# A new hand-written order for the last part of layer two, with one more wait between the halves of a bank

## The chip, the core and the metric

The kernel runs on one core of one Trainium2 chip. The metric is the device time of one execution in microseconds. The median of three runs before the change is 786.66 us (784.89 to 787.54).

## The reference

The kernel computes one inference step of a two-layer decoder trunk for a prompt of 512 tokens and a group of 8 x 4 sample tokens that share all weights. Layer one mixes tokens by dilated sliding-window attention; layer two, where the change lies, by a matrix-state recurrence (RWKV-7). Both layers also attend to 256 memory tokens, gate the branches and project them out. Cut to layer two:

```python
p = xn @ w_in                                   # one input projection
cols, q_mem, gate = split(p)
xs = cols + mu * (prev(cols) - cols)            # token shift
r, k, v, w, a = heads(xs)                       # 12 heads of 64
for t in tokens:                                # per head, state S is 64 x 64
    sa = S @ a_t
    S = S * w_t + outer(sa, b_t) + outer(v_t, k_t)
    y_t = S @ r_t
y = group_norm(y) + (r * k * r_k).sum() * v
h = concat([y, cross_attention(q_mem)]) * silu(gate)
out = x + rms_norm(h @ w_out)
```

## The kernel before

All arithmetic is in 32 bits. A large product is made as three matmuls of a high and a low part: `hi` is a rounded copy of the weights (ScalarE, line 328), `lo` the rest (GpSimd, line 329).

The recurrence of layer two is worked in chunks of 64 tokens, 8 chunks, for three groups `g` of four heads. For one group the steps are these.

- Scores, and then `products` (line 1506, `P2` for the last group): a triangular inverse by elimination. VectorE makes 30 steps of two operations, an outer product `TX` (line 1557) and its addition to `T` in PSUM (line 1559). Steps 1 to 7 of the last group belong to the part ahead; steps from 8 on (`HOLD`) belong to the part that the change orders. After steps 12 and 22 a small square `n` for the sample tokens (line 1541) is put in. After step 30, `T` is transposed on VectorE (line 1569), two small products `X` (lines 1579 and 1589) complete the inverse, and `w`, `q` and `v` (lines 1600 and 1615) apply it.
- `Chunks(2)` (`C`): for chunk c, `inputs` (line 1789) multiplies the state by the chunk's columns (`z`) and VectorE adds the result to `UV` (line 1795); `state` (line 1801) makes the next state `St` (`z` again, then VectorE at line 1812), with `Sd`, the decayed state, from GpSimd (line 1799).
- `outputs` (`Y`): y of two chunks at a time, in two halves that write one PSUM bank: a first half of few matmuls for i = 0, 2, 4, 6 and a second half for i = 1, 3, 5, 7 (`y_of`, line 1760). The matmuls of a second half wait for a VectorE operation of the step that follows the first half (line 1779).
- `block` (`N0`, `N1`, `N2`): the group norm of the y just made (`yc`, `gst`, transposes `gn` by TensorE, `bv`) and the gate (`ug`, line 1929, then `h` on ScalarE and GpSimd).

Beside it stand the output projections. `earlier` (`F`) makes the products `o` of the first four feature blocks, 16 products of six 128x512 matmuls (by half, token tile and group) and sample products `o100s` to `o111s`; VectorE adds each to `z` (lines 2134 and 2139). `F` steps left over from `crossed` come first. `weights` (`W`) splits the weight pieces, `inner` (`U`) gates two more blocks, `residuals` (`R`) transposes the residual (`x`, line 2001; ScalarE copies it out at line 2002). `last` (`O0` to `O3`) makes the last products of a token tile, squares them (line 2033), scales (line 2040) and adds the residual (line 2045); `last_sample` (`L`) does it for the sample rows (`o20s`, `o21s`, `zS`). `S2` and `M2` are the sample tokens of the last group.

What sets the order: up to this part a planner (`Flow.run`) does. From there on `Flow.close` takes the next step of the stream that the written list `CLOSE` names, and each of TensorE, VectorE, ScalarE and GpSimd executes its instructions in that order. Each engine takes its own queue in order, so an instruction that waits holds up all behind it. A stream may `yield` the name of an event, and the list has to reach that event first. The products share two PSUM banks (`mm`), as do the residual transposes; the small products, the norms' transposes and the sample steps share one bank (`q`).

Of the kernel before, what the change touches and what calls it, by code (L numbers as in the profile page):

```python
# [13 lines left out]
SYNC = DependencyInfo(DependencyClass.Sync, DependencyReason.DATA)  # L14
# [39 lines left out]
PRELOAD = ()  # L54
MULT = 'GGGGGGDD'
LOWER = 'GGGGGG'
CLOSE = 'F F F W1 W1 W1 P2 P2 P2 P2 F P2 P2 P2 F P2 R R F F W W P2 F F P2 F F P2 F F P2 P2 R W P2 W1 P2 R R F W1 W1 U U U W W P2 R F P2 F P2 U U P2 F P2 F P2 F F P2 W W F P2 F W F F R P2 F F P2 W W P2 F F P2 F F F P2 P2 F P2 P2 P2 P2 W W P2 F P2 P2 C C C F C C S2 S2 S2 F F Y Y Y Y C Y Y Y C W F C C Y Y W W F C Y Y Y N0 N0 C N0 F C F F Y Y Y N0 F C C Y Y Y N0 N1 N1 C F N0 N1 F C N0 N0 N1 F N1 C N1 Y Y Y F F N0 N0 N0 C C N1 N1 Y Y Y S2 N2 N2 O0 O0 O0 N1 N2 S2 O1 O1 O1 O0 N2 O1 S2 O0 N1 N1 S2 S2 O1 O0 O0 O1 S2 O2 O2 O2 S2 N2 O2 O1 O0 O0 S2 O2 O2 O0 O0 O1 O1 S2 S2 O1 O1 R M2 R N2 O2 N2 N2 R N2 R R N2 N2 M2 O2 O1 C O2 O0 O2 O2 M2 M2 L L L L O3 O3 O3 O3 O1 O1 O3 O3 L L O2 O2 O2 O3 O3 O3 L L O3 O3 L C C L L L O0 O0 O3 O3 O3 L L'
YB = [[[0, 4], [4, 8]], [[0, 4], [4, 8]], [[0, 4], [4, 6], [6, 8]]]
QUARTERS = (1, 1), (0, 0), (1, 0), (0, 1)
QO = (0, 2, 1, 3)  # L60
# [122 lines left out]
class Flow:  # L183
# [47 lines left out]
    def close(self):  # L231

        with self.tc.manual_schedule(engines={ET.PE, D, A, G}):
            for name in CLOSE.split():
                s = next(s for s in self.streams if s.name == name)
# [19 lines left out]
def _device(tc, I, O):  # L255
# [32 lines left out]
    def ps_zs(name):  # L288
        return psum[0].tile([128, 1024], F32, tag="zs", bufs=1, name=name)

    def ps_c(tag, name, bufs=1):
        return psum[0].tile([128, 512], F32, tag=tag, bufs=bufs, name=name)
# [419 lines left out]
    with ExitStack() as pro:  # L712
# [44 lines left out]
        for j, g in enumerate(GORD):  # L757
            a = 1152 + 32 * j
# [259 lines left out]
    half = {}  # L1018
# [189 lines left out]
    flow = Flow(tc)  # L1208
# [92 lines left out]
    def unit(c, j, h):  # L1301
        a = ((c - j) % 8 // 2 * 2 + h) * 64
        return H2[(c + j) % 2], slice(a, a + 64)


    def turned(c, j, h):
        return h ^ (c + j) % 2

    def score(c, j, h):
        a = ((c - j) % 8 // 2 * 2 + turned(c, j, h)) * 64  # L1310
        return H2[(c + j) % 2], slice(a, a + 64)
# [350 lines left out]
    def add_affine(p, src, cols, shape):  # L1662
        o_ = bvs[p][:, cols]
        o_ = o_.rearrange("p (c t) -> p c t", t=64) if shape else o_
        nc.vector.scalar_tensor_tensor(o_, src, vec("lnw", p), o_, ALU.mult, ALU.add)
# [80 lines left out]
    class Chunks:  # L1746

        def __init__(self, g):
            self.g, self.st = g, sts[g]
            self.states, self.c, self.yps, self.norms, self.fence, self.n, self.ops = [], 0, None, [], False, 0, []  # L1750
            self.St = rw.tile([128, 2, 64], F32, tag="St", bufs=4, name=f"St{g}i")
            nc.vector.memset(self.St, 0.0)
            self.states.append(self.St)
            self.zs = ps_zs(f"z{g}").rearrange("p (e k c v) -> p e k c v", k=2, c=4, v=64)
# [5 lines left out]
        def y_of(self, cs, e):  # L1760


            g, (AR, SR, UV, u) = self.g, (self.st.AR, self.st.SR, self.st.UV, self.st.u)
            a, b = [ab for ab in YB[g] if ab[0] <= cs[0] < ab[1]][0]
            if cs[0] == a and e:
                self.yps = ps_c("y", f"y{g}_{a}")
            yps = self.yps
            steps = [(c, k, t) for c in cs for k in range(3) for t in range(2) if (c or k) and (k == 0 and t) == e]
            for step in steps:
                c, k, t = step  # L1770
                for j, h in PAIRS:
                    if turned(c, j, h) == t:
                        r, s = score(c, j, h)
                        lhs = SR[r, 2 - k, j, s] if k else AR[H2[h], j, 1, CH[c]]
                        rhs = (UV[r, 1, j, unit(c, j, h)[1]] if k == 1 else u[r, c, t] if k else self.states[c][H2[h], j ^ h])
                        y = ((c - a) * 2 + h) * 64
                        self.put(yps[r, y:y + 64], lhs, rhs, e and step == steps[0], not e and step == steps[-1])
                        if not e and self.fence:
                            tc.add_manual_dep(flow.last(), self.ops[self.begun if g == 2 else -1].name, SYNC, reason="one half of a bank")
            c = cs[1]  # L1780
            if not e and c == b - 1:
                def out(pt):
                    pt = pt[:, 0:(b - a) * 128].rearrange("p (c j t) -> p c j t", j=2, t=64)
                    for j in range(2):
                        add_affine(2 * g + j, pt[:, :, j], slice(64 * a, 64 * b), True)

                self.norms.append(norm(g, yps, 2 * (b - a), f"_{b}", out, self.fence))
# [306 lines left out]
    def closing():  # L2094
# [65 lines left out]
        def outputs():  # L2160
            yield "chunks"
            C = out.chunks
            for i in range(8):
                c = i + 1
                yield f"step{2 * c - 2 + c % 2}"
                if i % 2:
                    yield f"step{n + 1}"
                else:
                    if [i] == [b for _, b in YB[2] if b == i]:
                        yield f"read{i}"  # L2170
                n = C.n
                if c % 2:
                    C.begun = n
                C.y_of((c - 1, c) if c % 2 else (c - 2, c - 1), c % 2 == 1)
                flow.done(f"turn{i}")
                yield
# [17 lines left out]
        flow.spawn(0, inner(), name="U")  # L2194
        flow.spawn(0, earlier(), name="F")
        flow.spawn(0, outputs(), name="Y")
        for i, (a, b) in enumerate(YB[2]):
            flow.spawn(0, block(i, a, b), name=f"N{i}")
# [103 lines left out]
```

## Time and profile before

| | |
|---|---|
| median of 3 runs | 786.66 us |
| profiled execution, its own time | 787.78 us |
| its span | 785.9 us |
| granted TensorE clock over the span | 0.986 |
| TensorE busy | 744.5 us, 95% |
| VectorE busy | 448.0 us, 57% |
| GpSimd busy | 354.4 us, 45% |
| ScalarE busy | 342.0 us, 44% |

Times in rows of the profile are microseconds from the start of the span. A row of the timeline has start, length, engine, line, operation, what it writes and reads, and in brackets how long the engine stood idle before it and which instruction ended that. PE is TensorE, DVE is VectorE, ACT is ScalarE, POOL is GpSimd. The part that the list orders fills about the last 110 us.

### The profile page before, as it was taken

The page shows a single profiled execution, that of the slowest core. Times are in us where ns is not written, and L with a number is a line of the kernel's source. Part 1 is how long each engine was busy: PE and PEld are TensorE (multiplying, and loading weights), DVE is VectorE, ACT ScalarE, POOL GpSimd, SP SyncE. Part 2 cuts the span into 40 slices and gives each one's busy share as a digit, 9 for nine tenths or more (in the row PEclk, how much of TensorE's full clock was granted, in tenths as well). Part 3 has the DMA queues.
Part 4 walks back from the last instruction along what each step waited for, and adds up shares of the span by engine and source line. Part 5 has one row for each costly group of instructions (what it writes and reads, how often), then busy time and mean ns, then how long its engine had stood idle before and what let it go on. Part 6 is the DMA issues. An engine that isn't in the chain of part 4 may idle for free.

```text
span 785.9 us, 20504 instructions
## 1 busy us (share of the span) xinstructions
PE 744.5 (95%) x8457; PEld 622.5 (79%) x8457; DVE 448.0 (57%) x1076; ACT 342.0 (44%) x807; POOL 354.4 (45%) x385
## 2 busy tenths in 40 slices
PE   6899999999999999999999999999999999989894
PEld 5877868888986877798888889888897888657763
DVE  7733321216646376662444679644799457777566
ACT  7554321214554364447585358223644242533122
POOL 4642322332240393655443338533855444333465
PEclk9999999999999999999999999899999999999997
DMA  7465358872133772263114522201222341622003
GB/s 254 126 204 200 108 172 278 318 279 98 63 116 117 250 233 75 69 198 103 54 49 148 166 80 80 71 16 33 80 73 83 112 112 56 185 93 84 17 15 132
DMA packets 58785, 98.21 MB, mean 125 GB/s; under 512 B 7775, under 2 KB 23039, under 8 KB 58655
## 3 DMA queue, kind: packets, MB, share of 16 engines
q1 hardware_dynamic: 58692, 96.91, 37.7%
q8 instruction: 66, 1.08, 0.6%
q14 instruction: 27, 0.22, 0.1%
HBM read 83.39 MB, written 13.49 MB: 123 GB/s over the span
## 4 chain that ended last, share of the span: by engine, by line
PE 67%; DVE 15%; POOL 5%; DMA 5%; ACT 3%; issue 3%; SPq 0%; DVEq 0%; POOLq 0%; ACTq 0%
PE o L1941 3%; PE Sx L591 2%; PE b_h L337 2%; PE y L1757 2%; PE b_h L336 2%; PE b_h L338 2%; DVE TX L1557 1%; PE z L1757 1%; PE sc L1473 1%; PE ox L615 1%; DMA raw_a<-in_w_in_a 1%; PE o L832 1%; PE ptx L607 1%; DVE T L1559 1%; PE w L1600 1%
## 5 line engine op out<-in xcount | busy, mean ns | idle before, releaser
L329 POOL TENSOR_TENSOR lo_a<-raw_a,hi_a 128x512 fp32r<-128x512 f32 x44 | 56.9, 1295 | 124.1 <-ACT hi_a L328 123.4
L329 POOL TENSOR_TENSOR lo_b<-raw_b,hi_b 128x512 fp32r<-128x512 f32 x58 | 78.5, 1354 | 73.4 <-ACT hi_b L328 62.4
L328 ACT CAST hi_a<-raw_a 128x512 fp32r<-128x512 f32 x44 | 27.3, 620 | 64.3 <-DMA raw_a<-in_w_in_a 36.5
L328 ACT CAST hi_b<-raw_b 128x512 fp32r<-128x512 f32 x58 | 36.4, 628 | 31.8 <-issue 9.9
L336 PE MATMUL b_h<-xg,hi_b 128*128 128x272 f32 x160 | 47.9, 300 | 0.0
L337 PE MATMUL b_h<-xg,lo_b 128*128 128x272 f32 x160 | 47.2, 296 | 0.0
L338 PE MATMUL b_h<-xg,hi_b 128*128 128x272 f32 x160 | 47.1, 295 | 0.0
L1941 PE MATMUL o<-hi_o,h 128*128 128x512 f32 x96 | 36.0, 426 | 2.9 <-DVE z L2134 2.3
L337 PEld LDWEIGHTS b_h<-xg,lo_b 128*128 128x128 f32 x160 | 30.1, 188 | 2.3 <-issue 1.9
L1559 DVE TENSOR_TENSOR T<-T,TX 128x30 f32<-128x30 f32 (+14 forms) x90 | 30.1, 335 | 2.2
L336 PEld LDWEIGHTS b_h<-xg,hi_b 128*128 128x128 f32 x160 | 30.1, 188 | 1.3 <-ACT hi_b L328 0.4
L1557 DVE TENSOR_TENSOR TX<-T,TT 128x30 f32<-128x30 f32 (+14 forms) x90 | 29.2, 325 | 3.3 <-ACT T L1528 1.7
L338 PEld LDWEIGHTS b_h<-xg,hi_b 128*128 128x128 f32 x160 | 30.1, 188 | 0.9 <-issue 0.5
L1941 PEld LDWEIGHTS o<-hi_o,h 128*128 128x128 f32 x96 | 18.8, 196 | 9.3 <-DVE z L2134 2.8
L329 POOL TENSOR_TENSOR lo_o<-raw_o,hi_o 128x512 fp32r<-128x512 f32 x12 | 15.7, 1316 | 22.1 <-ACT hi_o L328 14.8
L1799 POOL TENSOR_TENSOR Sd<-St,DF 128x128 f32<-128x128 f32 x21 | 8.9, 422 | 36.6 <-DVE St L1812 25.0
L1941 PE MATMUL o<-lo_o,h 128*128 128x512 f32 x48 | 19.7, 411 | 0.9 <-POOL lo_o L329 0.9
L1382 POOL TENSOR_TENSOR rv<-rv,mhalf 128x10 f32<-128x10 f32 x6 | 14.2, 2374 | 13.8 <-DVE rv L1381 7.7
L1473 PE MATMUL sc<-AR,BK 64*64 64x128 f32 x384 | 18.4, 278 | 1.9 <-DVE bv L1419 0.9
L824 ACT COPY PT<-pa 128x512 f32<-128x512 f32 x16 | 9.0, 586 | 18.7 <-PE pa L823 14.7
L1933 POOL TENSOR_TENSOR h<-ug,h 128x128 fp32r<-128x128 f32 (+3 forms) x11 | 9.1, 838 | 17.1 <-ACT h L1932 17.0
L1473 PEld LDWEIGHTS sc<-AR,BK 64*64 64x64 f32 x384 | 12.6, 132 | 5.2 <-issue 1.8
(1112 smaller groups left out, 2732.3 us busy)
## 6 DMA issues: line engine op xcount, KB each, us to landing
raw_b<-in_w_in_b SPq DMA_DIRECT2D x58, 256.0 KB, 2.9
raw_a<-in_w_in_a SPq DMA_DIRECT2D x44, 256.0 KB, 2.9
kc<-in_kc SPq DMA_DIRECT2D x18, 512.0 KB, 6.3
vc<-in_vc SPq DMA_DIRECT2D x18, 512.0 KB, 6.9
raw_o<-in_w_out_b SPq DMA_DIRECT2D x16, 256.0 KB, 2.6
out_win<-t SPq DMA_DIRECT2D x12, 272.0 KB, 3.4
x<-in_x SPq DMA_DIRECT2D x8, 272.0 KB, 5.2
xr<-in_x SPq DMA_DIRECT2D x16, 136.0 KB, 4.1
```

Source lines behind the costliest of these rows:

```text
L328: nc.scalar.copy(hi, raw)
L329: lo_eng.tensor_tensor(lo, raw, hi.bitcast(F32), ALU.subtract)
L336: nc.tensor.matmul(ps[:, :n], hi, xh, start=first, stop=False)
L337: nc.tensor.matmul(ps[:, :n], lo, xh, start=False, stop=False)
L338: nc.tensor.matmul(ps[:, :n], hi, xl, start=False, stop=last)
L591: nc.tensor.matmul(S[hh][64 * e:64 * e + 64, 0:256], qm[r, f, a:a + 64], kT[l][r, f, :], start=True, stop=True)
L1382: nc.gpsimd.tensor_tensor(rv[:, 1], rv[:, 0], mhalf.to_broadcast([128, 10]), ALU.pow)
L1473: nc.tensor.matmul(pts[e][unit(c, j, h)[0], a:a + 128], BK[H2[h], j, x, CH[c]], AR[H2[h], j, :, CH[c]], start=True, stop=True)
L1557: nc.vector.tensor_tensor(pd, TP[:, 0:s, s:s + 1].to_broadcast([128, s, w]), TT[:, s:s + 1, s + 1:32].to_broadcast([128, s, w]), ALU.mult)
L1559: nc.vector.tensor_tensor(TP[:, 0:s, s + 1:32], TP[:, 0:s, s + 1:32], pd, ALU.add)
L1757: nc.tensor.matmul(out, lhs, rhs, start=start, stop=stop)
L1941: nc.tensor.matmul(ps, x, w, start=begun is None and i + k == 0, stop=i == len(hs) - 1 and k == 2)
```

## The change

The list `CLOSE` is written in another order. It has the same steps, and three more `Y`: `outputs` now also yields once before the first halves for i = 2, 4 and 6, until the step after the last second half is in the list. With it goes a new wait: the matmuls of these first halves wait for the VectorE operation of that step (`ended`), as those of the second halves already do (`begun`).

```diff
-CLOSE = 'F F F W1 W1 W1 P2 P2 P2 P2 F P2 P2 P2 F P2 R R F F W W P2 F F P2 F F P2 F F P2 P2
...
+CLOSE = 'W1 W1 P2 P2 P2 P2 P2 P2 P2 P2 P2 P2 P2 P2 P2 P2 W1 P2 F F F F P2 P2 P2 F F W1 F
...
-            self.states, self.c, self.yps, self.norms, self.fence, self.n, self.ops = [], 0, None, [], False, 0, []
+            self.states, self.c, self.yps, self.norms, self.fence, self.n, self.ops, self.ended = [], 0, None, [], False, 0, [], None
...
-                        if not e and self.fence:
-                            tc.add_manual_dep(flow.last(), self.ops[self.begun if g == 2 else -1].name, SYNC, reason="one half of a bank")
+                        if self.fence and not (e and self.ended is None):
+                            op = self.ops[(self.ended if e else self.begun) if g == 2 else -1]
+                            tc.add_manual_dep(flow.last(), op.name, SYNC, reason="one half of a bank")
...
                 if i % 2:
                     yield f"step{n + 1}"
-                else:
+                elif i:
+                    yield f"step{n + 1}"
+                    C.ended = n
                     if [i] == [b for _, b in YB[2] if b == i]:
                         yield f"read{i}"
```

Where instructions move, engine by engine. The changed file has up to three lines more, so L1757 to L1779 keep their numbers, and L1941, L1950, L2134 and L2001 are L1942, L1951, L2135 and L2002 in it.

VectorE in the elimination, before: steps 11 to 14 (a step is the row pair L1557, L1559; the last numbers count the step and its width), the add of the first output product (`z<-z,o`) and the copy of the first small square.

```order
L1559 TENSOR_TENSOR T_8643<-T_8643,TX_8637 128x11x20
L2134 TENSOR_TENSOR z_8986<-z_8986,o_9153 128x512
L1557 TENSOR_TENSOR TX_8637<-T_8643,TT_8636 128x228
L1559 TENSOR_TENSOR T_8643<-T_8643,TX_8637 128x12x19
L1548 COPY TX_8637<-n_9175 32x64
L1557 TENSOR_TENSOR TX_8637<-T_8643,TT_8636 128x234
L1559 TENSOR_TENSOR T_8643<-T_8643,TX_8637 128x13x18
L1557 TENSOR_TENSOR TX_8637<-T_8643,TT_8636 128x238
L1559 TENSOR_TENSOR T_8643<-T_8643,TX_8637 128x14x17
L2134 TENSOR_TENSOR z_8987<-z_8987,o_9186 128x512
```

VectorE in the elimination, now, around the place where the first add stands: steps 20 to 22, with the norm's multiply (`yc`) and the sample square's addition (`SAs`).

```order
L1557 TENSOR_TENSOR TX_8637<-T_8643,TT_8636 128x220
L1559 TENSOR_TENSOR T_8643<-T_8643,TX_8637 128x20x11
L1642 TENSOR_TENSOR yc_8_8309<-yc_8_8309,gst_8_8308 128x512
L1557 TENSOR_TENSOR TX_8637<-T_8643,TT_8636 128x210
L1559 TENSOR_TENSOR T_8643<-T_8643,TX_8637 128x21x10
L2135 TENSOR_TENSOR z_8986<-z_8986,o_9194 128x512
L1557 TENSOR_TENSOR TX_8637<-T_8643,TT_8636 128x198
L1559 TENSOR_TENSOR T_8643<-T_8643,TX_8637 128x22x9
L1546 TENSOR_TENSOR SAs_7543<-SAs_7543,n_9204 32x64 x2
```

The first add stood behind step 11 and stands behind step 21 now; the multiply stood ahead of step 8. Between step 8 and the transpose stood eight adds of 128x512, two of 128x128 and the gates of two blocks; now there are five and one, no gate, and the multiply.

TensorE at the start of the recurrence, before: `v`, the first state's `z`, a sample product, and the next `inputs` and `state` with nothing between them.

```order
L1615 MATMUL v_9620<-UV_7540,SA_7538 64x64 x16
L1757 MATMUL z_9640<-UV_7540,BK_6994 64x64 x8
L1950 MATMUL o110s<-hi_o_9373,xsm 32x128 x4
L1950 MATMUL o110s<-lo_o_9374,xsm 32x128 x4
L1950 MATMUL o110s<-hi_o_9399,xsm 32x128 x4
L1950 MATMUL o110s<-lo_o_9400,xsm 32x128 x4
L1757 MATMUL z_9640<-St_0_9649,AR_6993 64x64 x4
L1757 MATMUL z_9640<-UV_7540,BK_6994 64x64 x8
L1682 MATMUL q2s<-UVs_7542,SAs_7543 32x64 x4
```

TensorE there, now: the third of four output products that stand in the first steps, between `inputs` (reads `St_0`) and `state` (reads `BK`).

```order
L1757 MATMUL z_9568<-St_0_9577,AR_6993 64x64 x4
L1942 MATMUL o_9606<-hi_o_9375,h_9118 128x512
L1942 MATMUL o_9606<-lo_o_9376,h_9118 128x512
L1942 MATMUL o_9606<-hi_o_9375,h_9118 128x512
L1942 MATMUL o_9606<-hi_o_9526,h_9118 128x512
L1942 MATMUL o_9606<-lo_o_9527,h_9118 128x512
L1942 MATMUL o_9606<-hi_o_9526,h_9118 128x512
L1757 MATMUL z_9568<-UV_7540,BK_6994 64x64 x8
```

The four output products of the second group's first half stood ahead of `w`, around the two `X`; all four now stand behind `v`.

TensorE at its end, before: residual transposes (`x`, `x1s`), the last state's `z`, and the first of the last two token products.

```order
L2001 MATMUL x_10176<-ident,x1SA 128x128 x4
L2007 MATMUL x1s<-ident,last 32x128 x8
L1757 MATMUL z_9640<-UV_7540,BK_6994 64x64 x8
L1651 MATMUL gn2s<-ident,yc2s 64x64 x2
L1941 MATMUL o_10231<-w2h,h_9118 128x512
L1941 MATMUL o_10231<-w2l,h_9118 128x512
```

TensorE at its end, now: the last token product's end, then transposes, then the sample products.

```order
L1942 MATMUL o_10200<-w2h,h_9118 128x512
L1651 MATMUL gn2s<-ident,yc2s 64x64 x2
L2002 MATMUL x_10215<-ident,x1BK 128x128 x4
L2002 MATMUL x_10221<-ident,x1SA 128x128 x4
L2008 MATMUL x1s<-ident,last 32x128 x8
L1951 MATMUL o20s<-w2h,xsm 32x128 x4
```

Before, five of the eight groups of residual transposes stood ahead of `w`; now all eight stand behind `v`, two of them and `x1s` between the last token product and the sample products.

More of the change, by code (lines that the diff above doesn't have):

```diff
@@ L56 @@
 LOWER = 'GGGGGG'
-CLOSE = 'F F F W1 W1 W1 P2 P2 P2 P2 F P2 P2 P2 F P2 R R F F W W P2 F F P2 F F P2 F F P2 P2 R W P2 W1 P2 R R F W1 W1 U U U W W P2 R F P2 F P2 U U P2 F P2 F P2 F F P2 W W F P2 F W F F R P2 F F P2 W W P2 F F P2 F F F P2 P2 F P2 P2 P2 P2 W W P2 F P2 P2 C C C F C C S2 S2 S2 F F Y Y Y Y C Y Y Y C W F C C Y Y W W F C Y Y Y N0 N0 C N0 F C F F Y Y Y N0 F C C Y Y Y N0 N1 N1 C F N0 N1 F C N0 N0 N1 F N1 C N1 Y Y Y F F N0 N0 N0 C C N1 N1 Y Y Y S2 N2 N2 O0 O0 O0 N1 N2 S2 O1 O1 O1 O0 N2 O1 S2 O0 N1 N1 S2 S2 O1 O0 O0 O1 S2 O2 O2 O2 S2 N2 O2 O1 O0 O0 S2 O2 O2 O0 O0 O1 O1 S2 S2 O1 O1 R M2 R N2 O2 N2 N2 R N2 R R N2 N2 M2 O2 O1 C O2 O0 O2 O2 M2 M2 L L L L O3 O3 O3 O3 O1 O1 O3 O3 L L O2 O2 O2 O3 O3 O3 L L O3 O3 L C C L L L O0 O0 O3 O3 O3 L L'
+CLOSE = 'W1 W1 P2 P2 P2 P2 P2 P2 P2 P2 P2 P2 P2 P2 P2 P2 W1 P2 F F F F P2 P2 P2 F F W1 F P2 W W P2 F P2 P2 F F F W P2 W1 W1 P2 F F P2 F F F P2 F R R F P2 F W W W W F F P2 P2 F U U U P2 P2 U U P2 P2 F F W P2 P2 P2 C C C W W F F F F F C F F C F Y Y Y Y W W C F Y Y Y C F C C S2 S2 S2 W Y Y Y C R F F C Y Y Y W W C N0 N0 R F Y Y Y Y C C Y Y Y N0 C F F N0 N0 F N1 N1 F F N0 N1 C F F N1 C F N0 N0 F F Y Y Y Y C C Y Y Y S2 N0 N0 N0 N1 R S2 N2 N2 N2 R C S2 R N2 N1 O1 O1 O1 N1 N1 N2 S2 N1 C C O0 O0 O0 N2 S2 O1 N2 N2 N2 N2 N2 O0 O0 O0 S2 O1 S2 O0 O0 O0 N1 N1 O1 O0 O0 O1 S2 O2 O2 O2 S2 S2 O1 O2 O2 O2 O1 O1 O1 M2 R O2 O2 O3 O3 O3 O2 M2 O3 O3 O2 O2 O3 M2 M2 R R R R O1 L L L L O2 O3 L O2 O2 O3 O3 O0 O0 O0 L L L L O3 O3 L O1 O1 L O3 L O3 O3 L L'
 YB = [[[0, 4], [4, 8]], [[0, 4], [4, 8]], [[0, 4], [4, 6], [6, 8]]]
```

## The prediction

> **What bounds the kernel now.** I read the page first, then the busy time by windows over the last 110 us, then the chain of waits, then the timeline of VectorE and TensorE there.
>
> ```profile
> span 785.9 us, 20504 instructions
> PE 744.5 (95%) x8457; PEld 622.5 (79%) x8457; DVE 448.0 (57%) x1076; ACT 342.0 (44%) x807; POOL 354.4 (45%) x385
> ```
>
> TensorE is the full engine: 785.9 - 744.5 = 41 us of the whole span are free on it. The windows (columns: engines' busy us, granted clock, DMA share, GB/s) cut the closing part at four events: the first `w` matmul, the end of `v`, the end of `w2s`, and TensorE's last matmul but one group.
>
> ```profile
> core 0: us, PE busy (x) PEld busy (x) DVE busy (x) ACT busy (x) POOL busy (x), PEclk, DMA share, GB/s
> 676.00:722.18 46.18, 40.79 (x415) 29.01 (x414) 36.18 (x79) 17.88 (x38) 20.40 (x18) 0.96 0.38 112
> 722.18:728.00 5.82, 5.79 (x199) 5.65 (x200) 2.12 (x4) 1.69 (x3) 0.51 (x1) 1.00 0.02 6
> 728.00:751.23 23.23, 20.53 (x469) 16.16 (x464) 14.16 (x39) 3.83 (x8) 10.05 (x14) 1.00 0.05 13
> 751.23:775.60 24.37, 23.38 (x270) 15.52 (x266) 17.70 (x42) 10.21 (x33) 18.32 (x20) 1.00 0.16 59
> 775.60:785.90 10.30, 0.59 (x2) 0.50 (x2) 4.66 (x10) 0.51 (x2) 3.34 (x5) 0.60 0.39 141
> ```
>
> Free on TensorE are 5.39 us before `w`, 0.03, 2.70 in the recurrence, 0.99 after it, and 9.71 of tail. A new order moves no work off TensorE, so it can only win from these 18.8 us. Why TensorE has gaps before `w` is in VectorE's timeline:
>
> ```profile
> 682.22 0.34 DVE L1559 TENSOR_TENSOR T<-T,TX 128x168 f32<-128x168 f32 x1
> ...
> 685.03 0.33 DVE L1557 TENSOR_TENSOR TX<-T,TT 128x184 f32<-128x184 f32 x1
> ...
> 692.42 0.69 DVE L2134 TENSOR_TENSOR z<-z,o 128x512 f32<-128x512 f32 x1 [4.18 <-PE o L1941]
> ...
> 695.21 0.41 DVE L1559 TENSOR_TENSOR T<-T,TX 128x238 f32<-128x238 f32 x1
> 695.53 0.68 DVE L2134 TENSOR_TENSOR z<-z,o 128x512 f32<-128x512 f32 x1
> 696.12 0.40 DVE L1557 TENSOR_TENSOR TX<-T,TT 128x240 f32<-128x240 f32 x1
> ...
> 703.86 0.77 DVE L1929 SCALAR_TENSOR_TENSOR ug<-bv,pv,ug 128x544 f32<-128x544 f32 x1
> 704.55 0.35 DVE L1557 TENSOR_TENSOR TX<-T,TT 128x198 f32<-128x198 f32 x1
> ...
> 706.95 1.72 DVE L1929 SCALAR_TENSOR_TENSOR ug<-bv,pv,ug 128x544 f32<-128x544 f32 x1
> 708.59 0.32 DVE L1557 TENSOR_TENSOR TX<-T,TT 128x168 f32<-128x168 f32 x1
> ...
> 714.55 2.09 DVE L1569 STREAM_TRANSPOSE TX<-T 128x1024 f32<-128x1024 f32 x1
> ```
>
> The elimination (L1557/L1559 in pairs, steps 8 to 30) runs from 685.03 to the transpose at 714.55, 29.52 us. In it VectorE stands 4.18 us waiting for the first output product, because that product's add is ahead of the next step in its order. Nothing of `X`, `w`, `q`, `v` and the recurrence can start before the transpose. Behind it the chain of waits is TensorE's:
>
> ```profile
> 713.75 3.03 PE o L1941 x12
> 716.78 1.13 PE X L1579 x64
> 717.91 1.60 PE o L1941 x6
> 719.52 1.13 PE X L1589 x64
> 720.65 1.60 PE o L1941 x6
> 722.25 1.84 PE w L1600 x62
> ```
>
> **The change, part by part.** (1) The elimination. It may now start when the step before it ends, at 682.22 + 0.34 = 682.6, since the `yc` multiply is moved from before step 8 to behind step 20. The 23 steps cost what they cost. Of the 29.52 us the wait of 4.18 goes, for the first add comes after step 21: by the pace of the rows (29.52 - 4.18 = 25.34 with all that is mixed in) VectorE gets there about 695, and the product was ready at 692.42. Three of eight 128x512 adds leave the stretch: with one, the next row starts 0.91 after a step's start (695.21 to 696.12) where its 0.41 would do, so 0.5 each, 1.5. The two gate rows leave: 704.55 - 703.86 = 0.69 and 708.59 - 706.95 = 1.64, together 2.3. One add a quarter as wide leaves, 0.1 as an estimate from the 0.5. `yc`, as wide as the adds, comes in: 0.6. So 25.34 - 1.5 - 2.3 - 0.1 + 0.6 = 22.0, and the transpose starts at 704.6 instead of 714.55, **9.9 us earlier**. TensorE can keep up: the five products that stay inside need 1.5 each (3.03 for two), and the adds that free their banks are farther apart than that.
>
> From the transpose to `w` the same four pieces follow as in the chain above (X, a product, X, now the sample product); 722.25 - 714.55 = 7.7 stays. `w` starts near 712.4.
>
> (2) What this lead is worth. TensorE's work is the same, so what was done before `w` and now is not must be paid later: four output products, 3.03 + 1.60 + 1.60 = 6.2, and five residual transposes of 0.49, the step between two in a row:
>
> ```profile
> 699.92 0.65 PE L2001 MATMUL x<-ident,x1SA 128*128 128x128 f32 x4
> 700.41 0.60 PE L2001 MATMUL x<-ident,x1BK 128*128 128x128 f32 x4
> ```
>
> Together 8.7. Net of it the lead at `w` is 9.9 - 8.7 = **1.2 us**: the rest is only moved.
>
> (3) The recurrence. The moved products stand between its steps, where TensorE now waits for VectorE:
>
> ```profile
> 731.78 0.68 PE L1757 MATMUL y<-UV,SR 64*64 64x64 f32 x16 [0.41 <-DVE UV L1795]
> ...
> 736.51 0.33 PE L1757 MATMUL y<-St,AR 64*64 64x64 f32 x4 [0.48 <-DVE St L1812]
> ...
> 742.64 0.33 PE L1757 MATMUL y<-St,AR 64*64 64x64 f32 x4 [0.49 <-DVE UV L1795]
> ...
> 749.57 0.33 PE L1757 MATMUL y<-St,AR 64*64 64x64 f32 x4 [0.48 <-DVE UV L1795]
> ```
>
> Of the 2.70 us free, three of these waits stay, since in the new order again an `inputs` step stands right ahead of the second half of y in 1, 5 and 7; in 3 a state step and a transpose lie between. 3 x 0.45 = 1.35 stays, **1.35 us** is won.
>
> (4) The added wait. It makes the first half of y in 2, 4 and 6 wait for a VectorE operation of the step after the last half. In all three places that is the state which these matmuls read themselves or an earlier one (St_2, St_4, St_5 against St_2, St_4, St_6), so nothing is queued behind it longer than before: 0. It can gain nothing, as it removes nothing. If I misread the index, it costs at most a wait like that at 736.51 in each: 3 x 0.48 = 1.4.
>
> (5) After `w2s`. The late transposes share two banks with the last products, and ScalarE must copy them out, which it had done early for five of eight. The trace does not show these waits. From below: none, 0, if the products between cover them. From above: one ScalarE copy per late transpose in a row at the end, two of 0.6 in front of the last sample products. I take half, **-0.6 us**, as one of the two has other work beside it.
>
> (6) The tail, in the chain:
>
> ```profile
> 773.40 1.05 PE o20s L1950 x32
> ...
> 774.68 1.00 DVE z L2045 x2
> ...
> 776.33 0.60 DVE z L2040
> 776.93 0.21 DVE zS L2064
> ...
> 779.14 0.74 DVE z L2045
> ...
> 780.54 0.40 DVE zS L2076
> ```
>
> TensorE's part of the sample rows ends at 775.6, but VectorE comes to their add (`zS`) at 776.85 to 776.93, after residual adds. In the new order transposes stand between the last token product and the sample products, so VectorE has 1.5 us more (two transposes of 0.49 and `x1s`, estimated at one more) to clear those adds. I take **+1.1**: the 1.3 us delay goes, less a little for the transposes' own residual adds; the bounds are 0 and 2.1 (also the two adds between 779.14 and 780.54).
>
> Sum: 1.2 + 1.35 + 0 - 0.6 + 1.1 = 3.05 us, made against the profiled execution: its time 787.78, span 785.9. 784.7 would follow there. That execution lies 1.1 above the median 786.66 of the three runs, so I forecast **783.6**.
>
> POOL is a cost on the side: the second gate row took 1.64 where the first took 0.69, and GpSimd was at work beside it:
>
> ```profile
> 706.81 1.28 POOL L329 TENSOR_TENSOR w2l<-raw_o,w2h 128x512 fp32r<-128x512 f32 x1
> ```
>
> The Trainium skill, GPSIMD Engine Reference, section Specifications, says that GpSimd and VectorE share SBUF interfaces and collide where a VectorE operation has two SBUF inputs; these rows agree. By that rule the second gate row, now between `w` and `q`, where GpSimd has casts queued, delays the copy that `v` waits for by an estimated 0.3, and the sum would be 2.75; by the quick row it is 3.05.
>
> **The rivals.** A: the order only moves work. The lead of 1.2 stays, the recurrence stalls as before, and ScalarE's copies cost the full 1.2 at the end with no gain in the tail: 0, so 786.7. For it: 8.7 of 9.9 us are plainly moved. Against: 2.70 us of free time with products now placed in it.
>
> B: the half clock, slower. TensorE is thinner in the elimination now, with waits for the adds. The trace has one such place:
>
> ```profile
> 704.00:708.00 4.00, 2.35 (x13) 1.85 (x14) 3.87 (x9) 1.76 (x4) 2.50 (x2) 0.74 0.12 34
> 708.00:712.00 4.00, 3.97 (x19) 2.87 (x21) 3.77 (x10) 1.29 (x3) 2.54 (x3) 0.83 0.49 135
> ```
>
> With TensorE busy 2.35 of 4 us the clock fell to 0.74 and 0.83, that is 2 x 4 x (0.26 + 0.17) = 3.4 us at half speed. From 695 to 712.4 TensorE has now 0.5 (the norm's transposes, as the residual ones) + 6 x 1.5 + 2 x 1.05 (sample products, as o20s) + 2 x 1.13 = 13.9 us of work in 17.4. At half clock throughout that is 27.8, `w` comes 10.4 later, and the whole is 10.4 - 3.05 = 7.35 slower: 794.0. It decides from about 13 us at half clock (half of it, less 3.5 of slack, equals the gain); 3.4 us would be lost in the slack. The Trainium skill, TensorE: Matmul & The Clock Gate, section Why this matters for your kernels, sets the limit at idle gaps of about 3 us. My longest gap is an estimated 1.8 us, so by the page no drop comes; the trace dropped earlier than the page says, and it decides, so B keeps a chance.
>
> C: the added wait bites after all: 1.4 of the 3.05 go, 785.0. The order list speaks against it.
>
> D: all cover works: 1.2 + 2.70 + 0 + 2.1 = 6.0, so 780.7.
>
> **How the numbers follow.** Forecast case 0.51, A 0.26, B 0.10, C 0.05, D 0.08. What a measurement of this kernel tells from no change is about 0.3%, 2.4 us: below 784.3 is faster, above 789.0 slower. Faster: forecast and D, 0.59. Same: A and C, 0.31. Slower: B, 0.10. The range goes from D, 780.7, to A with the upper half-spread of the runs (787.54 - 786.66 = 0.9), 787.5; B lies outside. The forecast's own range is 781.6 (tail and recurrence at their better ends, halved) to 785.0.
>
> **What would show it.** Right: the transpose L1569 near 705, `w` near 712.4, no VectorE wait of 4 us on `o`; about 1.3 us free on TensorE between `v` and `w2s`; the last `zS` add near 777.5 to 778. Wrong: `w` earlier than 717 but the end unchanged (A: look at TensorE's free time after `w2s`, with ScalarE copies as releasers); a granted clock under 0.9 over 695 to 712 (B); y rows waiting for St in 2, 4 or 6 (C). A difference ahead of 670 us would make the whole account wrong, since nothing is changed there.

## The result, and the profile after

The changed kernel takes 782.06 us (median of 8 runs, 779.90 to 784.18) against 786.65 us for the kernel before (median of 8, 784.89 to 788.59). The ratio is 0.9942, with a 95% interval of 0.9923 to 0.9961: 4.6 us faster, between 3.1 and 6.1. The prediction had 783.6 us, 3.05 us faster, and a range of 780.7 to 787.5. The profiled execution of the changed kernel took 780.78 us; its page:

```profile
span 778.8 us, 20497 instructions
...
PE 738.3 (95%) x8457; PEld 617.4 (79%) x8457; DVE 447.7 (57%) x1076; ACT 342.2 (44%) x807; POOL 353.7 (45%) x385
```

The two profiled spans differ by 7.1 us, more than the medians. Part of that lies ahead of the changed part and is not the change's: in the execution of before the granted clock fell to half for about 7 us in a place that both kernels have in common.

```profile
504.00:508.00 4.00, 4.00 (x23) 3.36 (x21) 1.23 (x4) 0.58 (x1) 2.22 (x1) 0.57 0.24 81
508.00:512.00 4.00, 4.00 (x81) 3.76 (x82) 0.75 (x2) 1.31 (x2) 0.15 (x1) 0.58 0.02 4
```

So the traces are compared from an event that the change does not touch: the last matmul of the input projection (`b_h`, L338). It, the end of `v`, the last matmul of the sample products (`o21s`) and the last operation of VectorE, in the timelines of before and after:

```profile
670.77 0.29 PE L338 MATMUL b_h<-xg,hi_b 128*128 128x272 f32 x1
...
727.92 0.23 PE L1615 MATMUL v<-UV,SA 64*64 64x64 f32 x2
...
775.17 0.40 PE L1950 MATMUL o21s<-w2l,xsm 128*32 128x128 f32 x8
...
780.46 0.48 DVE L2076 SCALAR_TENSOR_TENSOR zS<-zS,rvls,last 128x256 f32<-128x256 f32 x1
```

```profile
668.50 0.29 PE L338 MATMUL b_h<-xg,hi_b 128*128 128x272 f32 x1
...
715.77 0.22 PE L1615 MATMUL v<-UV,SA 64*64 64x64 f32 x2
...
769.42 0.40 PE L1951 MATMUL o21s<-w2l,xsm 128*32 128x128 f32 x8
...
773.34 0.47 DVE L2077 SCALAR_TENSOR_TENSOR zS<-zS,rvls,last 128x256 f32<-128x256 f32 x1
```

In us, the first stretch counted from the start of that `b_h`, with the 8.7 us of moved work (four output products, five transposes) taken off where it is done now:

| stretch | before | after | difference | without the moved work | forecast |
|---|---|---|---|---|---|
| last `b_h` to the end of `v` | 57.38 | 47.49 | -9.89 | -1.19 | -1.2 |
| end of `v` to the end of `o21s` | 47.42 | 53.83 | +6.41 | -2.29 | -1.35 + 0.6 |
| end of `o21s` to VectorE's last end | 5.37 | 3.99 | -1.38 | -1.38 | -1.1 |
| sum | 110.17 | 105.31 | -4.86 | -4.86 | -3.05 |

The sum agrees with the 4.6 us of the medians. The windows of after, cut at the same events as those of before (`w`, here its third matmul, the end of `v`, the end of `w2s`, the end of `o21s`):

```profile
core 0: us, PE busy (x) PEld busy (x) DVE busy (x) ACT busy (x) POOL busy (x), PEclk, DMA share, GB/s
674.00:710.07 36.07, 30.79 (x367) 21.46 (x367) 31.43 (x73) 12.65 (x27) 14.05 (x14) 1.00 0.33 94
710.07:715.90 5.83, 5.81 (x200) 5.67 (x202) 3.58 (x7) 3.22 (x7) 4.37 (x4) 1.00 0.51 141
715.90:743.70 27.80, 26.55 (x497) 20.97 (x492) 14.38 (x37) 5.23 (x10) 11.02 (x14) 1.00 0.16 41
743.70:769.84 26.14, 24.55 (x280) 17.10 (x280) 18.78 (x48) 12.95 (x38) 19.66 (x24) 1.00 0.15 55
769.84:778.80 8.96, 0.38 (x2) 0.30 (x2) 3.98 (x9) 0.51 (x2) 2.65 (x3) 0.64 0.45 161
```

TensorE is free for 1.25 us in the recurrence, where it was free for 2.70, and for 1.59 us behind it, where it was 0.99. VectorE's timeline shows the elimination without a wait, from step 8 to the transpose. The chain shows that what follows the transpose is much as before, one product between the two `X`, and a sample product ahead of `w` (not in the chain) where a product stood; the first two matmuls of `w` start at 709.53, the rest wait 0.22 us for ScalarE's copy of `X`:

```profile
680.76 0.35 DVE L1557 TENSOR_TENSOR TX<-T,TT 128x184 f32<-128x184 f32 x1
...
693.09 0.68 DVE L2135 TENSOR_TENSOR z<-z,o 128x512 f32<-128x512 f32 x1
...
702.45 2.07 DVE L1569 STREAM_TRANSPOSE TX<-T 128x1024 f32<-128x1024 f32 x1
```

```profile
701.67 3.07 PE o L1942 x12
704.74 1.13 PE X L1579 x64
705.87 1.59 PE o L1942 x6
707.46 1.15 PE X L1589 x64
...
710.07 1.87 PE w L1600 x60
```

All waits of TensorE in the recurrence that are left, and the first half of y in 2, which now carries the added wait and shows none. The three that are left stand ahead of the second halves of y in 1, 5 and 7, as the prediction had it:

```profile
723.84 0.68 PE L1757 MATMUL y<-UV,SR 64*64 64x64 f32 x16 [0.39 <-DVE UV L1796]
726.90 0.39 PE L1757 MATMUL y<-St,AR 64*64 64x64 f32 x6
732.73 0.33 PE L1757 MATMUL y<-St,AR 64*64 64x64 f32 x4 [0.43 <-DVE UV L1796]
741.97 0.33 PE L1757 MATMUL y<-St,AR 64*64 64x64 f32 x4 [0.43 <-DVE UV L1796]
```

### The profile page after: what moved, and what is told of

It reads as the page before. It is cut to its first block, busy times and chain, and to the rows that moved or that the text cites. A ratio compares the mean times of both kernels' runs of the same rounds, so it can differ in the third digit from the quotient of the medians.

```text
span 778.8 us, 20497 instructions
## 1 busy us (share of the span) xinstructions
PE 738.3 (95%) x8457; PEld 617.4 (79%) x8457; DVE 447.7 (57%) x1076; ACT 342.2 (44%) x807; POOL 353.7 (45%) x385
## 4 chain that ended last, share of the span: by engine, by line
PE 68%; DVE 15%; DMA 5%; POOL 4%; issue 3%; ACT 3%; SPq 1%; DVEq 0%; POOLq 0%; ACTq 0%
PE o L1942 4%; PE y L1757 2%; PE Sx L591 2%; PE b_h L337 2%; PE b_h L336 2%; DVE TX L1557 2%; PE b_h L338 2%; PE z L1757 2%; DVE T L1559 2%; PE sc L1473 1%; PE ox L615 1%; PE o L832 1%; PE ptx L607 1%; PE sA L862 1%; PE so L917 1%
## 5 line engine op out<-in xcount | busy, mean ns | idle before, releaser
L338 PE MATMUL b_h<-xg,hi_b 128*128 128x272 f32 x160 | 47.1, 295 | 0.0
L1942 PE MATMUL o<-hi_o,h 128*128 128x512 f32 x96 | 35.1, 414 | 0.8 <-DVE z L2135 0.5
L1559 DVE TENSOR_TENSOR T<-T,TX 128x30 f32<-128x30 f32 (+14 forms) x90 | 30.1, 335 | 2.2
L1557 DVE TENSOR_TENSOR TX<-T,TT 128x30 f32<-128x30 f32 (+14 forms) x90 | 29.3, 325 | 3.3 <-ACT T L1528 1.6
L338 PEld LDWEIGHTS b_h<-xg,hi_b 128*128 128x128 f32 x160 | 30.1, 188 | 0.9 <-issue 0.5
L1942 PEld LDWEIGHTS o<-hi_o,h 128*128 128x128 f32 x96 | 18.0, 188 | 6.6 <-ACT z L1971 0.9
L1942 PE MATMUL o<-lo_o,h 128*128 128x512 f32 x48 | 19.2, 400 | 1.6 <-POOL lo_o L329 1.6
```

The costliest lines, as they stand in the source:

```text
L338: nc.tensor.matmul(ps[:, :n], hi, xl, start=False, stop=last)
L1557: nc.vector.tensor_tensor(pd, TP[:, 0:s, s:s + 1].to_broadcast([128, s, w]), TT[:, s:s + 1, s + 1:32].to_broadcast([128, s, w]), ALU.mult)
L1559: nc.vector.tensor_tensor(TP[:, 0:s, s + 1:32], TP[:, 0:s, s + 1:32], pd, ALU.add)
L1942: nc.tensor.matmul(ps, x, w, start=begun is None and i + k == 0, stop=i == len(hs) - 1 and k == 2)
```

## The experiments

Each was timed against the kernel before in the same set. The last four columns come from its trace, as in the table above. All but 2 carry the added wait.

| kernel | against before, us (95%) | `b_h` to `v` | `v` to `o21s` | `o21s` to end | sum |
|---|---|---|---|---|---|
| before | | 57.38 | 47.42 | 5.37 | 110.17 |
| after | -4.6 (-6.1 to -3.1) | 47.49 | 53.83 | 3.99 | 105.31 |
| 1: old order, added wait | -0.1 (-1.7 to +1.6) | 57.27 | 47.43 | 5.23 | 109.93 |
| 2: new order, no added wait | -3.8 (-5.4 to -2.1) | 47.50 | 53.83 | 3.99 | 105.32 |
| 3: new to `v`, old behind | -1.2 (-3.0 to +0.7) | 47.48 | 56.52 | 5.23 | 109.23 |
| 4: old to `v`, new behind | +2.8 (+1.1 to +4.5) | 57.36 | 49.99 | 4.01 | 111.36 |
| 5: adds later | +3.3 (+1.7 to +5.0) | 59.79 | 47.42 | 5.36 | 112.57 |
| 6: square and adds | 0.0 (-1.9 to +2.0) | 55.73 | 47.43 | 5.23 | 108.39 |
| 7: new, moved work in a block | -0.9 (-2.8 to +0.8) | 46.97 | 58.11 | 3.96 | 109.04 |
| 8: new, late transposes early | -1.8 (-3.1 to -0.5) | 47.62 | 55.41 | 5.14 | 108.17 |
| 9: new, other front | -3.2 (-4.4 to -2.0) | 48.73 | 53.25 | 4.83 | 106.81 |
| 10: new, other tail | -2.0 (-3.7 to -0.4) | 47.96 | 56.78 | 4.41 | 109.15 |
| 11: 9 and 10 | -1.1 (-2.7 to +0.6) | 47.67 | 55.97 | 4.04 | 107.68 |
| 12: new, smaller change of tail | -6.1 (-7.6 to -4.5) | 47.44 | 53.04 | 4.40 | 104.88 |

Up to the end of `o21s` the traces of before, 4, 5, 7, 10 and 11 hold a fall of the granted clock, or two (4 and 10), of 3.4 us at half clock each. One adds at most 1.7 us to a sum, and next to nothing where VectorE sets the pace: before and 4 have one ahead of `v` and 1, with the same order there, has none (57.38, 57.36 and 57.27 us).

**1 and 2: the added wait alone, and the new order without it.**

```diff
-C C Y Y W W F C Y Y Y N0
+C C Y Y Y W W F C Y Y Y N0
...
+                        if self.fence and not (e and self.ended is None):
```

> The old order with the added wait alone (the three more Y stand right ahead of the first halves of y for 2, 4 and 6). My account: 0 us, since the matmuls of these halves wait for a state of the same step or a later one anyway; no y row of 2, 4 or 6 has a wait of its own that before lacks. Rival C: three waits of 0.48 us, 1.4 us slower than before, 788.1.

```diff
-                        if self.fence and not (e and self.ended is None):
-                            op = self.ops[(self.ended if e else self.begun) if g == 2 else -1]
+                        if self.fence and not e:
+                            op = self.ops[self.begun if g == 2 else -1]
```

> The new order without the added wait. My account: 0 us against the new order, so 782.1, since the three first halves have no wait of their own in its trace. Rival C: the wait costs up to 1.4 us, so up to 1.4 faster than the new order, 780.7.

The traces with and without it agree within 0.2 us in every stretch, 0.01 us in the new order. The wait costs nothing; rival C falls.

**3 and 4: the two halves of the new order, each with the other half old.** Against the list of the new order, the first place behind the elimination that differs, in 3 and in 4 (in 3 the rest follows the old list, in 4 all that is ahead does):

```diff
-P2 P2 P2 C C C W W F F F F F C F F C F Y
+P2 P2 P2 R R R R R F F W W F F F F F F W W F C C C F C C S2
```

```diff
-P2 P2 C C C W W F F F F F C F F C F Y Y Y Y W W C F
+P2 P2 C C C C C Y Y Y Y C Y Y Y C F
```

> The new order up to the end of v (the elimination ahead of the adds, five transposes and four output products taken out from before w); all that is left then follows in the order of before, so the moved transposes and products stand in one block right behind v, ahead of the recurrence. My account: the early transpose is only worth its net lead, 1.2 us as forecast or 1.45 as the two traces show; TensorE's waits in the recurrence stay near 2.7 us and the tail stays as before. 1.2 to 2.0 us faster than before, about 785.0. Rival 1, the early elimination is the whole gain: 4.6 us faster, 782.0. Rival 2, the order only moves work: 0, 786.7.

> The old order up to the end of v, and what is left in the new order: no output product is left over to stand between the first steps of the recurrence, but the late residual transposes and the end are as in the new order. My account: the tail gives 1.1 to 1.3 us, the late transposes cost 0.6, and the waits in the recurrence stay near 2.7 us: 0.5 to 1.3 us faster than before, about 785.8. Rival, the order behind v is the whole gain: 4.6 us faster, 782.0.

The front alone gives 1.2 us by an interval that includes 0, and 0.9 in the trace, against before: `v` ends as early as in the new order, 47.48 us, but `v` to `o21s` takes 56.52, that is 47.42 and the moved 8.7 and 0.4 of waits for the transposes' banks. The net lead is about what it was costed at. The second half alone is slower than before, 2.8 us by the medians and 1.2 in the trace, and there my account missed: it had the waits in the recurrence unchanged. Without products to stand between its steps the new order has more of them than the old one. Four follow one another at its start:

```profile
728.48 0.34 PE L1757 MATMUL z<-St,AR 64*64 64x64 f32 x8 [0.51 <-DVE St L1815]
729.24 0.46 PE L1757 MATMUL z<-UV,BK 64*64 64x64 f32 x16 [0.41 <-DVE UV L1796]
730.18 0.34 PE L1757 MATMUL z<-St,AR 64*64 64x64 f32 x8 [0.38 <-DVE St L1813]
730.95 0.68 PE L1757 MATMUL y<-UV,SR 64*64 64x64 f32 x16 [0.42 <-DVE UV L1796]
```

All waits from `v` to `o21s` come to 5.61 us here, 3.56 before and 2.83 after. The tail is the new one, 4.01 us. So 2.05 us more of waits less 1.36 of tail make 0.7 us of the trace's 1.2, and the fall of the clock behind `v` can be the other 0.5. The medians differ by 1.6 more; the runs of 4 have a mean granted clock of 0.988 and those of before beside them 0.990, which points the same way, but no trace shows where that time lies.

**5 and 6: the elimination's wait by itself.** The old order with the first adds later (5); then the small square and steps 8 to 17 ahead of the first product as well (6).

```diff
-F F F W1 W1 W1 P2 P2 P2 P2 F P2 P2 P2 F P2 R R F F W W P2 F F P2 F F P2 F F P2 P2
+F F F W1 W1 W1 P2 P2 P2 P2 P2 P2 P2 P2 P2 P2 P2 F F P2 R R F F W W P2 F F P2 F F
```

```diff
-F F F W1 W1 W1 P2 P2 P2 P2 F P2 P2 P2 F P2 R R
+W1 W1 W1 P2 P2 P2 P2 P2 P2 P2 P2 P2 P2 P2 F F F F F P2 R R
```

> The old order in all but one thing: the first output product's add stands behind step 18 of the elimination instead of behind step 11, and the adds and small steps that stood between steps 12 and 22 follow it closely, so that the 4.18 us wait of VectorE for the first output product should go. My account: TensorE has its work ahead of w all the same, so only its gaps that waited for VectorE there can go (0.66, 0.60 and 1.65 us, 2.9 together): w 1 to 2.9 us earlier, and the whole 1 to 2.9 us faster, about 784.7. Rival, the wait of VectorE is itself on the path: w 4.2 us earlier, 4.2 us faster, 782.5. Rival 2, TensorE bounds the stretch wholly: 0.

> The old order with the elimination's steps 8 to 17 and the small square between them ahead of the first output product on every engine, the first add behind step 17 as in the run before (which was said to be step 18 there); all else as there. In that run VectorE's wait of 4.18 us for the first product came back as one of 3.56 us for the small square, which stood behind the product on TensorE, and TensorE then waited 3.65 us for the late first add. Here both should be gone: VectorE reaches the first add when the product is ready. My account: w 1 to 2.9 us earlier than before against the first sample product o00s (TensorE's gaps of 0.66, 0.60 and 1.65 us for VectorE), the whole 1 to 2.9 us faster than before, about 785.0. Rival 1, the elimination is the path: w 4.2 us earlier, 4.2 us faster, 782.5. Rival 2, the adds behind step 17 bring TensorE new waits of the same size: 0.

5 is 3.3 us slower than before instead of 1 to 2.9 faster: the wait changed hands. VectorE's timeline, then TensorE's:

```profile
693.33 0.21 DVE L1548 COPY TX<-n 32x64 f32<-32x64 f32 x1 [3.56 <-PE n L1541]
...
697.76 0.68 DVE L2135 TENSOR_TENSOR z<-z,o 128x512 f32<-128x512 f32 x1
```

```profile
698.49 0.50 PE L1942 MATMUL o<-hi_o,h 128*128 128x512 f32 x1 [3.65 <-DVE z L2135]
```

VectorE no longer waits for the product but for the small square, which stands behind that product in TensorE's order. It then comes to the first add only at 697.76, and as only two banks hold products, the third product waits for that add. (The first add stands behind step 17 there, not 18 as the expectation says.) In 6 TensorE's wait for the add is gone and VectorE's for the product is down to 0.92 us:

```profile
693.67 0.69 DVE L2135 TENSOR_TENSOR z<-z,o 128x512 f32<-128x512 f32 x1 [0.92 <-PE o L1942]
```

The transpose comes 1.64 us earlier against the last `b_h` (42.05 against 43.69 in 1), `w` 1.56 us, and the trace gains 1.54 us against that of 1. Part of what could be won goes to a wait of TensorE for the `lo` half of a weight piece from GpSimd, 1.55 us where it is 0.43 in 1. So by the trace the elimination is worth the gaps of TensorE that it frees, 1 to 2.9 us by my account, and not the 4.18 us of rival 1; the medians (0, between 1.9 faster and 2.0 slower) fit with the 1.5, but can't tell it from the nothing of rival 2.

**7 and 8: what the moved work does where it stands.** In 7 the four products and two transposes stand in one block; in 8 the last transposes stand together.

```diff
-P2 P2 P2 C C C W W F F F F F C F F C F Y
+P2 P2 P2 R R W W F F F F F F F W W F F C C C C C Y
```

> The new order, but the four output products and two residual transposes that it places between the first steps of the recurrence stand in one block right behind v, ahead of the recurrence; all else, the end too, as in the new order. My account now (the kernel with only the order behind v new had 5.1 us of waits on TensorE between v and the end of o21s where the new order has 2.8): the waits come back, 2.0 to 2.6 us slower than the new order, about 784.4, that is 2.3 faster than before. Rival, the place of the products makes no difference once they are behind v: as the new order, 782.1.

```diff
-M2 R O2 O2 O3 O3 O3 O2 M2 O3 O3 O2 O2 O3 M2 M2 R R R R O1 L L L L
+M2 R R R R R O2 O2 O3 O3 O3 O2 M2 O3 O3 O2 O2 O3 M2 M2 O1 L L L L
```

> The new order, but the last residual transposes (two x and x1s) stand directly behind the one before them, ahead of the third token tile's last two products, instead of between those products and the sample products. My account of the tail: VectorE comes late to the sample rows' add again (1 us behind the end of o21s instead of 0.3), and TensorE's wait of 0.63 us for ScalarE's copy of a transpose goes: 0.4 to 1.1 us slower than the new order, about 782.8. Rival, the late transposes only cost: 0.6 to 1.2 us faster than the new order, 781.2.

Both show the mechanism, larger than I had it. In 7 the waits come back (5.36 us from `v` to `o21s`), and `v` to `o21s` takes 58.11 us instead of 53.83. One part of these 4.3 us is a fall of the clock that came in the thin stretch, 3.4 us at half clock (2 x 4 x (0.29 + 0.13)), worth at most 1.7:

```profile
728.00:732.00 4.00, 3.31 (x80) 2.99 (x84) 0.80 (x3) 0.00 (x0) 0.73 (x2) 0.71 0.02 4
732.00:736.00 4.00, 3.50 (x104) 2.79 (x98) 1.35 (x5) 1.40 (x3) 1.06 (x2) 0.87 0.00 0
```

So the place of the products between the steps is worth 2.6 to 4.3 us in this stretch. In 8, 2.9 us of the new order's gain are lost in the trace (108.17 against 105.31), where I had expected 0.4 to 1.1. The late adds of VectorE are there (`zS` takes `o21s` 1.41 us behind its end, 0.26 in the new order), but the larger part is ahead of them:

```profile
772.24 0.43 PE L1951 MATMUL o20s<-w2h,xsm 128*32 128x128 f32 x8 [1.91 <-ACT xsm L1932]
```

```profile
773.80 0.40 PE L1951 MATMUL o21s<-w2l,xsm 128*32 128x128 f32 x8
...
775.61 0.28 DVE L2065 TENSOR_TENSOR zS<-zS,o21s 128x128 f32<-128x128 f32 x1
```

The same two places in the new order:

```profile
767.87 0.43 PE L1951 MATMUL o20s<-w2h,xsm 128*32 128x128 f32 x8 [0.61 <-ACT xsm L1932]
...
770.08 0.27 DVE L2065 TENSOR_TENSOR zS<-zS,o21s 128x128 f32<-128x128 f32 x1
```

The late transposes stand where TensorE waits for the gate of the sample rows. In the new order that wait is 0.61 us, with the transposes earlier it is 1.91.

**9 to 12: looking for a better order.** TensorE still has 1.82 us of wait ahead of the norm's transposes, and VectorE works without a gap over the last 8.6 us. 9 changes the front, 10 the tail (there the residual adds of a tile wait only for that tile's transposes), 11 both, 12 the tail again, more gently, with the sample rows' multiply on VectorE. (10 to 12 also mark each tile's transposes as done by an event of their own, let the sample rows wait for all transposes only in their last step, and put `sss` in the bank of the small products.)

```diff
-P2 P2 P2 P2 P2 P2 W1 P2 F F F F P2 P2 P2 F F W1 F P2 W W P2 F
+R R P2 P2 P2 P2 P2 P2 F F F F P2 F F W1 P2 P2 F P2 W W F F W1 P2 F F
...
-P2 F F P2 F F F P2 F R R F P2
+P2 P2 P2 R R P2 F F P2
```

> The new order with its elimination part rearranged: the first two output products' adds stand behind steps 20 and 21 and the norm's multiply behind them, so that the third and fourth product need not wait for the transposes of the norm (TensorE's wait of 1.82 us), the residual's loads are issued early, and two residual transposes stand ahead of VectorE's transpose instead of two behind w2s. My account: TensorE's free time ahead of w (4.3 us from o00s to v) can be filled at no cost as w waits for the elimination; two transposes of 0.5 to 0.6 us go from the path behind w2s: 1.0 to 1.2 us faster than the new order, about 781.0. Rival: in the new order these transposes fill waits of the sample steps of 0.2 to 0.3 us each, or the elimination is held up by the earlier adds: 0 to 0.5 us faster, 781.8.

```diff
-                yield "residuals"
+                yield f"residual{t}"
...
-O3 O3 O2 O2 O3 M2 M2 R R R R O1 L L L L O2 O3 L
+O3 O3 R O2 O2 O2 M2 O1 O1 O1 O3 O2 O2 M2 M2 L L L O3 R L O2 L
```

> The new order with another tail: the residual adds of the first two token tiles no longer wait in the list for the last transpose and stand ahead of the third tile's last products on VectorE, the gate of the sample rows stands ahead of the last product's add, the sample products directly behind one residual transpose, and the last two transposes behind them. My account: VectorE is busy without a gap from 765.19 to the end of the new order's profile (8.6 us), and TensorE waits 0.34, 0.63 and 0.61 us before the sample products; three to four adds of 0.74 us leave VectorE's last stretch and o21s ends up to 2 us earlier: 1.5 to 2.2 us faster than the new order, about 780.2. Rival: the outputs' transfers at the end, or GpSimd's multiply and power behind the sample rows, set the end: under 0.6 us faster, 781.8.

> Both of these rearrangements together. My account: the two places are apart, so the gains add: 2.5 to 3.4 us faster than the new order, about 779.2. Rival: with two transposes fewer behind w2s the sample steps or VectorE's adds set the pace there: no faster than the tail alone, 780.2.

```diff
-        nc.gpsimd.tensor_tensor(zs, zs, out.pS, ALU.mult)
+        nc.vector.tensor_tensor(zs, zs, out.pS, ALU.mult)
...
-O3 O3 O2 O2 O3 M2 M2 R R R R O1 L L L L O2 O3 L
+O3 O2 O3 M2 O3 O2 O2 O3 M2 M2 R L L L R O1 L O2 L
```

> The new order with a smaller rearrangement of its tail than the run before: the first token tile's two residual adds go into VectorE's gaps ahead of the third tile's products (behind the adds that free the product banks, not ahead of them, which in the run before made TensorE wait 2.27 us for the last add), the sample gate's copies stand ahead of ScalarE's copy of the last x transpose, the sample products ahead of x1s, and the multiply of the sample rows is on VectorE instead of GpSimd (0.4 against 1.17 us). My account: o21s ends 0.4 to 0.9 us earlier against the last input product than in the new order and the chain behind it is 0.7 us shorter: 0.6 to 1.5 us faster than the new order, about 781.0. Rival: VectorE, whose last adds take longer beside GpSimd's work, sets the end as before, and one of its adds moved early makes TensorE wait: 0 to 1 us slower than the new order, 782.5.

Three of the four missed, and the fourth fell short. 9 does what was said behind `v` (53.25 us for 53.83), but an add that I had placed too early made VectorE wait for its product inside the elimination, and the transpose came 1.4 us later (35.35 us behind the last `b_h`, 33.95 in the new order); the tail then took 4.83 us, so part of what TensorE gained seems to have waited for VectorE. The add in VectorE's timeline of 9:

```profile
701.55 0.69 DVE L2135 TENSOR_TENSOR z<-z,o 128x512 f32<-128x512 f32 x1 [0.83 <-PE o L1942]
```

In 10 the gates and residual adds that VectorE made ahead of the last product's add held its bank, and TensorE stood for 2.27 us; in 11 the same wait was 3.16:

```profile
772.19 0.43 PE L1951 MATMUL o20s<-w2h,xsm 128*32 128x128 f32 x8 [2.27 <-DVE last L2035]
```

12 keeps the adds that free banks ahead of everything else. `o21s` ends 0.84 us earlier than in the new order against the last `b_h` (100.48, 101.32), and the tail takes 4.40 us for 3.99: 0.43 us faster in the trace, less than expected. The multiply is shorter, but VectorE has to make it, and VectorE, which has no gap there, is the engine that sets the end:

```profile
771.64 0.42 DVE L2074 TENSOR_TENSOR zS<-zS,last 128x256 f32<-128x256 f32 x1
...
773.30 0.48 DVE L2078 SCALAR_TENSOR_TENSOR zS<-zS,rvls,last 128x256 f32<-128x256 f32 x1
```

Its median is 781.67 us (780.25 to 782.81, 6 runs), the lowest of all; its interval overlaps that of the new order, so that it is the better one rests on the trace.

## Why the prediction was right, point by point

**The elimination (1)** came out as worked: the transpose 9.83 us earlier against the last `b_h` (forecast 9.9), and the part of `w` that waits for `X` 9.84. Two small misses cancel in it: step 8 begins 2.0 us earlier where 2.4 had been taken, and from there to the transpose it takes 21.69 us instead of 22.0. The reason given for the 4.18 us was only half of it. "The first add comes after step 21" is not enough, as 5 shows: the small square has to stand ahead of the product on TensorE too, which the new list does by naming the `P2` steps first.

**The net lead (2)** was 1.2 us in the forecast and is 1.19 at the end of `v`. 3, which has nothing but this lead, gives 0.9 in its trace; its 1.2 by the medians can't be told from nothing.

**The recurrence (3)** and **the late transposes (5)** together were put at 0.75 us, and the stretch gives 2.29. The waits come out at 0.73: from `v` to `o21s` they fall from 3.56 to 2.83 us. In the recurrence they fall by 1.43 (forecast 1.35), with the three waits left where they were expected. Behind it they rise by 0.70 (forecast 0.6), but not for the reason given, so that the size of this term was luck. One transpose's wait for ScalarE's copy is in both traces (0.68 before, 0.63 after); new are 0.61 for the gate of the sample rows and 0.34 of a product for VectorE.

The rest, 1.56 us, is work that takes less time, where the prediction had said that a new order can only win from TensorE's free time. Summed over the rows of that stretch (each from its start to the next one's, less its wait), TensorE works 50.84 us where the old work and the moved 8.7 make 43.70 + 8.7 = 52.40. The mis-sized step is the price of work: I took the moved work at its old place, and all other work as unchanged. The four moved products cost 6.23 us there, and the twelve behind `v` 19.17, most of them single between smaller matmuls; all sixteen now take 24.59 us instead of 25.40: two in a row cost 2.98 us in the chain of after, two single ones 1.59 and 1.61.

```profile
716.22 2.98 PE o L1942 x12
...
719.48 1.59 PE o L1942 x6
...
721.46 1.61 PE o L1942 x6
```

The rows of y and the norms' transposes take 0.4 and 0.5 us less and the first sample products behind the gate (`o20s`) 0.3; the transposes of the residual 0.5 more. The moved work itself is thus only 0.3 us cheaper (0.8 on products, less 0.5 on transposes). The larger part is in rows that both orders have; fewer waits stand among them now, but no run shows that this is why. The account also took the waits of the old order for those that the new one would have without the products. 4 and 7 show that they would be 5.4 to 5.6 us: the steps of the recurrence stand closer in the new order, and it is the products between them that make this pay. The front by itself is worth about 1 us by its trace, the order behind it by itself is a loss (2.8 by the medians, 1.2 by the trace), and both together gain 4.6; the terms of my sum don't add up one by one.

**The added wait (4)** costs 0, as forecast, with and without the new order.

**The tail (6)** was put at 1.1 us and gives 1.38. The add of `o21s` starts 0.26 us behind its end where it started 1.28 behind. That the transposes there give VectorE time is right, but 8 shows that they also fill TensorE's wait for the sample gate, 1.3 us more, which the prediction had not seen.

**The gate rows.** They took 0.85 and 1.27 us, against 0.77 and 1.72 before. GpSimd was at work beside both of them, and the one of its operations that ran beside the first took 1.76 us where the one of the same form before it, `w2l`, took 1.28:

```profile
709.25 0.85 DVE L1930 SCALAR_TENSOR_TENSOR ug<-bv,pv,ug 128x544 f32<-128x544 f32 x1
709.47 1.76 POOL L329 TENSOR_TENSOR lo_o<-raw_o,hi_o 128x512 fp32r<-128x512 f32 x1
...
711.83 1.27 DVE L1930 SCALAR_TENSOR_TENSOR ug<-bv,pv,ug 128x544 f32<-128x544 f32 x1
```

That VectorE and GpSimd share SBUF interfaces (the Trainium skill, GPSIMD Engine Reference, section Specifications) agrees with these rows. From the third matmul of `w` (710.07) to the end of `v` TensorE has no wait and takes 5.9 us, where it took 6.0 before from the start of `w`, so the delay of 0.3 that the prediction drew from the page did not reach the path.

**The rivals.** A is excluded by the interval of the result. B did not come: the clock over 674 to 712 us of the trace was 1.00, with a wait of 1.82 us in it (the estimate was 1.8). C is excluded by 1 and 2. D, with all cover at work, had 6.0 us; the result lies between it and the forecast.

**The forecast's own range** was given as 781.6 to 785.0. Half of what the recurrence (1.35) and the tail (1.0) could still gain is 1.2 us, so its lower end should have been 782.4, and the 782.06 measured lies just under that.

## What to carry to other kernels

Price moved work where it will stand, and count the waits of the new order without it as well as with it: here the early chain was worth about 1 us by itself, the new order of the recurrence was a loss by itself, and only with independent products placed between the dependent steps did the two make 4.6 us. A wait that an add shows for its product is gone only when what its engine waits for next (here the small square) has been moved ahead of the product on the other engine too, and when the add still comes soon enough to free its bank. Put the operation that frees a bank ahead of other work of its engine, but not before its product is ready: three kernels here that put other work ahead of one (5, 10 and 11) gave time away, and so did 9, where one stood too early.

## What the runs showed of the hardware

Most of the scatter between runs of one kernel goes with the granted clock. Of 34 runs of the kernel before, timed beside experiments 1 and 3 to 5, the nine with a mean clock of 0.984 to 0.988 have a median of 789.8 us, the ten with 0.989 to 0.991 one of 786.6, and the fifteen with 0.992 to 0.994 one of 785.5. In the last 110 us, up to the end of `o21s`, the falls have one size: two neighbouring windows with 0.74 and 0.83 before, 0.77 and 0.80 and again 0.74 and 0.83 in 4, 0.71 and 0.87 in 7, each about 3.4 us at half clock. Most came where TensorE had gaps, though not in every execution (the one before at 704 us came again in 4, not in 1, which has the same order there). In 10 one came while TensorE was busy throughout, with transposes and small matmuls ahead of it.

```profile
748.00:752.00 4.00, 4.00 (x60) 3.56 (x59) 2.25 (x7) 1.78 (x5) 3.63 (x4) 0.72 0.06 18
752.00:756.00 4.00, 4.00 (x28) 2.56 (x28) 1.24 (x5) 1.14 (x4) 0.84 (x2) 0.85 0.00 0
```

The Trainium skill, TensorE: Matmul & The Clock Gate, section Why this matters for your kernels, names idle gaps above about 3 us as what brings the drop. The 3.65 us gap of 5 was followed by one (0.87 and 0.70 over 696 to 704 us) and the 3.16 us gap of 11 by another (0.78 and 0.79 over 768 to 776 us), which agrees. The fall of before came after waits of 0.60 and 1.65 us, and the first one in 10 had no wait of over 0.43 us in the 20 us ahead of it, which that section does not explain. What brought those stays open.
